# Another order of projections, and five set waits of the recurrence, in a two-layer hybrid decoder on one Trainium2 core

## The chip, the cores and the metric

The kernel runs on one core of one Trainium2 chip. TensorE (PE) multiplies matrices, VectorE (DVE), ScalarE (ACT) and GpSimd (POOL) work element by element, SyncE (SP) issues most of the transfers. The metric is the device time of one execution in microseconds, the median over several runs. Before the change it is 1106.13 us in three runs, from 1104.96 to 1108.74.

## The reference

Two layers work on x of 1024 positions by 1024 channels, both conditioned on one vector c. The first layer, in which the change lies, has one input projection whose columns feed two groups, and one output projection:

```python
p = h @ w_in                                  # r, k, v, w_lo, a_lo | u, v_g | z
# group A, 8 heads of 64: for each position t
sa  = S @ (-kk_t)
S   = S * w_t + sa (kk_t * a_t)^T + v_t k_t^T
y_t = S @ r_t                                 # then a layer norm per head, + bonus * v
# group B, 8 groups of 64: a spatial gate in chunks of 128 positions
y_b = u * (W_s @ layernorm(v_g) + b_s)
y   = concat(y_a, y_b) * silu(z) @ w_out
x   = x + gate * y
```

The second layer is attention in a window of 128 positions with its own projections, and a last RMSNorm follows.

## The kernel before

**Projections.** All weights and activations of the projections are split into a rounded part and a remainder, so that one tile of 128 output channels by 512 positions (a half of the sequence) takes 8 x 3 = 24 matmuls into one PSUM buffer, pproj. A column tile of the first layer is numbered: 0 to 3 are r of the head pairs 0 to 3, 4 to 7 are k, 8 to 11 are v, 12 the low-rank inputs of decay and a, 13 to 16 u, 17 to 20 the v of the spatial gate (called gv here), 21 to 24 the gate z of group A, 25 to 28 the gate of group B (zg). The stream (lines 989 to 1011) goes through them in the tuple ORDER (line 987), both halves of each, 24 matmuls a half. Tile 12 and pair 0 come ahead of it in the kernel's first part; three of their second halves open the stream, which makes 72 + 25 x 48 = 1272 matmuls. For the next tile in the order SP fetches the weights, ACT and POOL split them, while the one before is multiplied.

**Rooms.** After a half's matmuls the stream asks for room before the tile is evicted: r, k and v need fewer than 6 tiles held (line 981), z fewer than 2 waiting, gv fewer than 2 long-lived tiles, u fewer than 2. Where there is no room, the stream stands still. A unit (one head pair, one half of the sequence; eight of them, unit = 2 x pair + half) gives back its three tiles in front(): k behind the product with f, r behind AR, v behind bv.

**The recurrence's threads.** A unit runs through front (line 559: decay and low-rank products lw and la, the norm of kk by the transposes kt and kb, then BK, AR, SV, the transposes bkt and an, the bonus product bon), solve (line 664: products A, then on DVE a triangular solve of 15 steps that ends in ZT, then products p and pM with the steps M, Tq, M1), prep (line 776: products uw, mq and pn), scan (line 807: seven or eight hops of the state, product py) and post (line 834). front of a unit may begin when its r, k and v are there and solve of the unit before it has done its A products (line 1025). The spatial gate has its own thread, gm_tail (line 870: product gvn, a norm with vn on DVE, lnb, bst on DVE, product mix), and another thread accumulates the conditioning vectors of the second layer on DVE (adacc).

**Who sets the order on PE.** When the kernel is built, a planner (drive, line 1174) keeps a clock of its own. Each thread issues a few matmuls and then yields a time in microseconds: it may go on when the planner's clock has passed that time. The clock advances by a cost of each matmul, 512/2400 us for one of the stream. Among threads that are ready the lowest rank goes first: scan, then prep, solve and post, then front, gm_tail, the conditioning thread, and last the stream, which fills what is left; a debt lets the stream go first when the others have used much. The result is one fixed order of PE's instructions. On the chip PE executes it in that order and stands wherever an operand isn't ready. The waits of the threads are entries of the table LAT (line 58): 'unit_norm' between kt and kb, 'uw' between uw and mq, 'qt4' ahead of the product of N21 with Tq. Between la and kt, and between mq and pn, there is no wait. The instructions of the other engines are put in order by a scheduler with a model of times.

**What ends the stage.** When the stream is done and the other threads are nearly done, the output projection begins (out0_thread, line 1118).

Of the kernel before, what the change touches and what calls it, by code (L numbers as in the profile page):

```python
# [56 lines left out]

LAT = {"debt": 0.7, "share": 0.4, "p1": 2.31, "uw": 3.0, "mq": 4.0, "f0": 0.5, "sv0": 4.0, "wo": 2.31, "x1": 6.0, "yf": 7.85, "fetch": 3.85, "unit_norm": 12.0, "c81": 4.0, "qt1": 1.5, "bkt": 1.0, "qt2": 20.0, "qt3": 1.65, "qt4": 1.77, "qt5": 1.2, "qt6": 1.0, "yn": 12.0, "gm_tail1": 1.0, "gm_tail2": 12.0, "lnb": 1.0, "do_ada1": 4.5, "pick1": 0.5, "hop": 1.3, "ada": 8.0}

# [34 lines left out]
def tile_kernel(ctx, tc, x, cons, par, rows, ada, ada0, ew, wup, sgw, sgb, ewo, ow, owo, out, dbg=None):  # L94
# [43 lines left out]
    def pm(name):  # L138
        return ps.tile([P, HT], F32, name=name, tag="m", bufs=2)
# [419 lines left out]
    def front(un):  # L559
        j, half = un // 2, un % 2  # L560
# [26 lines left out]
        E2 = L  # L587
        S.activation(E2, L, AF.Exp, scale=KAPPA)
        pt = pm("kt")
        for b in range(4):  # L590
            transpose(pt[:, b * P:(b + 1) * P], kkn[:, b * P:(b + 1) * P], ident)
        sq = tmp("sqk")
        norm_scale(pt, sq, 1e-24, None, ALU.max, ALU.bypass, "k", rt)
        yield LAT["unit_norm"]
        pb = pm("kb")
# [30 lines left out]
        solvable[0] = un + 1  # L626
        yield LAT["f0"]
        SV = utile(un, [P, 8, 2, 64], "SV")
# [7 lines left out]
        S.activation(SV[0:64, 1:8:2, 1, :], pv4[64:128, :, 1, :], AF.Copy)  # L636
        yield LAT["c81"]
        BR = utile(un, [P, 8, 2, 2, 64], "BR")
        for g in range(2):
            pt = pm("bkt")  # L640
            for i in range(4):
                transpose(pt[:, i * P:(i + 1) * P], BK[:, g * 4 + i, :], ident)
            yield LAT["bkt"]
            S.activation(BR[:, g * 4:g * 4 + 4, :, 0, :], pt.rearrange("p (c e k) -> p c e k", c=4, e=2), AF.Copy)
        PA = utile(un, [P, 8, 2, 64], "PA")
        pt = pm("an")
        for i in range(4):
# [16 lines left out]
    def solve(un):  # L664
        AR, BK = us[un]["AR"], us[un].pop("BK")
        yield LAT["sv0"]
        yield lambda: scannable[0] > un
# [11 lines left out]
        for g in range(2):  # L679
            cg = slice(g * 4, g * 4 + 4)  # L680
            pts = [pm("A"), pM()]
            for i in range(4):
                c = g * 4 + i
                for hd in range(2):
                    hs = rows2[hd]
                    mm(pts[hd][:, i * P:(i + 1) * P], lhsT=BK[hs, c, :], rhs=AR[hs, :, c, :], start=True, stop=True)
            for hd in range(2):
                os = rows2[1 - hd]
                p4 = pts[hd].rearrange("p (c t) -> p c t", t=P)
                V.tensor_tensor(out=BR[:, cg, hd, 1, :], in0=p4[:, :, 64:128], in1=mr4, op=ALU.mult)  # L690
                V.tensor_tensor(out=AV[os, cg, :], in0=p4[os, :, 0:64], in1=ma4[os], op=ALU.mult)
                b0 = hd * 64
                for qd in range(2):
                    rows = slice(b0 + qd * 32, b0 + qd * 32 + 32)
                    ac = qd * 32
                    S.activation(Dgv[rows, cg, :, :], p4[rows, :, ac:ac + 32].rearrange("p c (b t) -> p c b t", b=2), AF.Copy)
                S.activation(N21[b0:b0 + 32, cg, :], p4[b0:b0 + 32, :, 32:64], AF.Copy)
            yield LAT["qt1"]

# [23 lines left out]
        Df = Dg.rearrange("p x t -> p (x t)")  # L723
        yield LAT["p1"]
        pt = pm("p1")
# [3 lines left out]
        S.activation(PA[:, :, 0, :], pt.rearrange("p (c v) -> p c v", c=8), AF.Copy)  # L729
        yield LAT["qt2"]  # L730
        p1 = pM()
# [6 lines left out]
        S.activation(M0, p1[:, 0:256].rearrange("p (c t) -> p c t", t=32), AF.Copy)  # L738
        yield LAT["qt3"]
        for c in range(8):  # L740
# [9 lines left out]
        for qd in range(4):  # L750
# [4 lines left out]
            else:  # L755
                S.activation(Z[rs, :, zc:zc + 32], Zq[rs], AF.Copy)
        yield LAT["qt4"]
        p1 = pM()
# [7 lines left out]
        S.activation(M1[96:128], p1v[96:128, :, 0:32], AF.Copy)  # L766
        yield LAT["qt5"]
        for c in range(8):
# [4 lines left out]
        S.activation(Z[64:96, :, 96:128], p1v[64:96, :, 32:64], AF.Copy)  # L773
        yield LAT["qt6"]

    def prep(un):
        u = us[un]
        AR, SV, BR, PA, dC = (u[k] for k in ("AR", "SV", "BR", "PA", "dC"))
        for g in range(2):
            cg = slice(g * 4, g * 4 + 4)  # L780
            pt = pm("uw")
            for i in range(4):
                mm(pt[:, i * P:(i + 1) * P], lhsT=Z[:, g * 4 + i, :], rhs=PA[:, g * 4 + i, :, :], start=True, stop=True)
            p4 = pt.rearrange("p (c a v) -> p c a v", c=4, a=2)
            S.activation(PA[:, cg, 1, :], p4[:, :, 1, :], AF.Copy)
            S.activation(SV[0:64, cg, 0, :], p4[0:64, :, 0, :], AF.Copy)
            S.activation(SV[64:128, cg, 1, :], p4[64:128, :, 0, :], AF.Copy)
        wdone[0] = un + 1
        yield LAT["uw"]
        for g in range(2):  # L790
            cg = slice(g * 4, g * 4 + 4)
            pt = pm("mq")
            for i in range(4):
                for e, hs in enumerate(rows2):
                    mm(pt[hs, i * P:(i + 1) * P], lhsT=PA[hs, g * 4 + i, 1, :], rhs=BR[hs, g * 4 + i, e, :, :], start=True, stop=True)
            p4 = pt.rearrange("p (c a v) -> p c a v", c=4, a=2)
            for e, hs in enumerate(rows2):
                V.tensor_tensor(out=Z[hs, cg, hs], in0=p4[hs, :, 0, :], in1=i2[hs].unsqueeze(1).to_broadcast([64, 4, 64]), op=ALU.add)
            V.tensor_tensor(out=AR[:, 1, cg, :], in0=p4[:, :, 1, :], in1=AR[:, 1, cg, :], op=ALU.add)
        pn = pm("pn")  # L800
        for c in range(8):
            for e, hs in enumerate(rows2):
                mm(pn[hs, c * 64:c * 64 + 64], lhsT=BR[:, c, e, 0, :], rhs=SV[:, c, e, :], start=True, stop=True)
        V.tensor_tensor(out=PA[:, :, 0, :], in0=pn.rearrange("p (c v) -> p c v", c=8), in1=dC.unsqueeze(2).to_broadcast([P, 8, 64]), op=ALU.mult)
        yield LAT["mq"]

    def scan(un):
        half, u = un % 2, us[un]
        AR, SV, BR, PA, dC = (u[k] for k in ("AR", "SV", "BR", "PA", "dC"))
        if half:  # L810
            V.tensor_copy(PA[:, 0, 1, :], Sst)
        else:
            V.tensor_copy(PA[:, 1, 1, :], PA[:, 0, 0, :])
        yield LAT["hop"]
        pc = psc("chain")
        for c in range(1 - half, 8 - half):
            yc = slice(c * 64, c * 64 + 64)
            mm(pc[:, yc], lhsT=Z[:, c, :], rhs=PA[:, c, 1, :], start=True, stop=True)
            if c == 7 - half:
                hopped[0] = un + 1  # L820
            V.scalar_tensor_tensor(out=PA[:, c + 1, 1, :] if c < 7 else Sst, in0=pc[:, yc], scalar=dC[:, c:c + 1], in1=PA[:, c, 0, :], op0=ALU.mult, op1=ALU.add)
            if c == 4:
                py = ps.tile([P, HT], F32, name="py", tag="y", bufs=1)
                for i in range(8):
                    for e, hs in enumerate(rows2):
                        mm(py[hs, i * 64:i * 64 + 64], lhsT=BR[:, i, e, 1, :], rhs=SV[:, i, e, :], start=i == 0, stop=False)
            if c < 7:
                yield LAT["hop"]
        for c in range(1 - half, 8):
            for hs in rows2:  # L830
                mm(py[hs, c * 64:c * 64 + 64], lhsT=AR[hs, 1, c, :], rhs=PA[hs, c, 1, :], start=False, stop=c == 7)
        return py

    def post(un, py):
        j, bv = un // 2, us[un]["bv"]
        sq = tmp("sqy", "tp", 2)
        norm_scale(py, sq, 1.0 / 64, LNX_EPS, ALU.mult, ALU.add, "y", lp)
        yield LAT["yn"]
        pb = pm("yt")
# [30 lines left out]
    def gm_tail(j, half, vT):  # L870
        if half == 0:
            gmc[j] = gm_consts(j)
        sgwt, lnb, bst = gmc[j]
        yield LAT["gm_tail1"]
        if half == 0:
# [14 lines left out]
        V.tensor_tensor(out=vg, in0=pv.rearrange("p (a d) -> p a d", d=64), in1=rs.unsqueeze(2).to_broadcast([P, 8, 64]), op=ALU.mult)  # L890
        yield LAT["gm_tail2"]
        yield lambda: (j, half) in gated_u
        if half == 0:
# [3 lines left out]
            V.tensor_tensor(out=bst, in0=pb[:, 0:P], in1=bst, op=ALU.add)  # L897
            yield LAT["lnb"]
        ut = gated_u.pop((j, half))
# [86 lines left out]

    ORDER = (21, 5, 1, 9, 17, 13, 6, 2, 22, 10, 25, 18, 7, 3, 23, 11, 14, 26, 24, 19, 15, 27, 20, 16, 28)

    def stream():
# [8 lines left out]
        while todo:  # L998
# [10 lines left out]
            if todo:  # L1009
                w = wn  # L1010
        done["h1"] = new_h()

    def prioritised(gen, offset):
# [468 lines left out]
```

## Time and profile before

| what | us |
|---|---|
| median of 3 runs | 1106.13 |
| the profiled execution, own time | 1109.73 |
| its span from first to last instruction | 1107.6 |
| PE busy | 1040.8 |
| DVE busy | 696.3 |
| ACT busy | 524.3 |
| POOL busy | 374.7 |

In the trace the first layer's overlapped stage, in which stream, recurrence and spatial gate share PE, lies from about 78 us to about 620 us from the span's start; the output projection of the first layer follows up to about 735 us, the second layer fills the rest. Times of instructions below are counted from the span's start. A row of a timeline is start, duration, engine, line, operation, output and inputs with the shape, how many instructions are merged in it, and in brackets how long the engine stood before it and what ended that. Matmuls overlap, so their pace is read from the distance of their starts.

### The profile page before, as it was taken

How to read it: one execution, taken by the hardware profiler on the slowest of the kernel's cores; microseconds unless marked ns; L12 is line 12 of the kernel's file. 1: busy time of each engine (PE TensorE's matmuls, PEld its weight loads, DVE VectorE, ACT ScalarE, POOL GpSimd, SP SyncE). 2: the span in 40 equal slices, each digit the busy share in tenths (PEclk: the TensorE clock that was granted, in tenths of full speed). 3: DMA queues.
4: the chain of work that ended last, by engine and by line, in shares of the span. 5: the costliest groups of instructions: out<-in, count | busy, mean ns of one | idle time of the engine just before them, and what ended most of it. 6: DMA issues, size and time to landing. Idle time of an engine off the chain costs nothing. (4 is left out here: it accounts for less than half of the span.)

```text
span 1107.6 us, 20700 instructions
## 1 busy us (share of the span) xinstructions
PE 1040.8 (94%) x7887; PEld 839.4 (76%) x7888; DVE 696.3 (63%) x1668; ACT 524.3 (47%) x1247; POOL 374.7 (34%) x483
## 2 busy tenths in 40 slices
PE   6989999999988898989999899999999999999997
PEld 3667778777776676766878777778888888878886
DVE  4455958586859485595642578864565654488754
ACT  4465555454454435445332233335565654487521
POOL 2333315141335122263423100134554544467201
PEclk9989999999999899999999899999999999999999
DMA  9501121212112121123122554421110111252121
GB/s 365 224 17 39 58 77 49 68 49 77 58 61 69 46 86 58 40 79 113 60 79 74 188 183 153 156 68 39 39 39 20 39 39 39 63 176 72 63 95 58
DMA packets 55131, 93.42 MB, mean 84 GB/s; under 512 B 5748, under 2 KB 15988, under 8 KB 55032
## 3 DMA queue, kind: packets, MB, share of 16 engines
q1 hardware_dynamic: 45176, 77.36, 21.3%
q10 hardware_dynamic: 9856, 14.75, 4.2%
q8 instruction: 62, 1.02, 0.4%
q14 instruction: 37, 0.30, 0.1%
HBM read 79.49 MB, written 12.59 MB: 83 GB/s over the span
## 5 line engine op out<-in xcount | busy, mean ns | idle before, releaser
L118 PE MATMUL pproj<-lo,whi 128*128 128x512 f32 x696 | 281.2, 404 | 0.0
L118 PE MATMUL pproj<-hi,whi 128*128 128x512 f32 x696 | 279.5, 402 | 0.7 <-ACT vt L1247 0.7
L118 PE MATMUL pproj<-hi,wlo 128*128 128x512 f32 x696 | 279.7, 402 | 0.0
L246 POOL TENSOR_TENSOR wlo<-wraw,whi 128x512 fp32r<-128x512 f32 x86 | 113.8, 1343 | 167.5 <-ACT whi L245 166.5
L118 PEld LDWEIGHTS pproj<-lo,whi 128*128 128x128 f32 x696 | 131.6, 189 | 24.9 <-issue 1.5
L118 PEld LDWEIGHTS pproj<-hi,whi 128*128 128x128 f32 x696 | 131.5, 189 | 24.5 <-ACT vt L1247 1.1
L118 PEld LDWEIGHTS pproj<-hi,wlo 128*128 128x128 f32 x696 | 131.3, 189 | 24.5 <-issue 1.2
L245 ACT ACTIVATE whi<-wraw 128x512 fp32r<-128x512 f32 x102 | 58.7, 622 | 65.9 <-PE htp L122 22.1
L118 PE MATMUL op<-wo,whi 128*128 128x512 f32 x256 | 82.2, 402 | 0.0
L1283 ACT ACTIVATE Sx<-Sx,nm 128x257 f32<-128x257 f32 (+1 forms) x128 | 62.3, 489 | 27.6 <-DVE nm L1279 25.5
L1279 DVE CUSTOM_DVE_ANT_0 Sx<-pS,bias,nsink 128x256 f32<-128x256 f32 (+1 forms) x128 | 53.4, 463 | 30.1 <-PE pS L118 28.6
L1287 POOL TENSOR_SCALAR Sx<-Sx,rc 128x256 f32<-128x256 f32 (+1 forms) x128 | 60.8, 492 | 25.4 <-DVE rc L1285 22.9
L1299 DVE TENSOR_TENSOR PL<-pT,PH 128x512 fp32r<-128x512 f32 (+1 forms) x64 | 41.6, 654 | 29.7 <-ACT PH L1298 29.2
L118 PEld LDWEIGHTS op<-wo,whi 128*128 128x128 f32 x256 | 49.0, 192 | 13.0 <-issue 2.1
L925 DVE SCALAR_TENSOR_TENSOR adacc<-araw,cond,adacc 128x512 f32<-128x512 f32 x56 | 44.0, 786 | 18.5 <-DMA araw<-ada 18.4
L118 PE MATMUL op<-hi,yh 128*128 128x512 f32 (+1 forms) x136 | 51.8, 381 | 0.4 <-ACT yh L1397 0.4
L118 PE MATMUL op<-hi,yl 128*128 128x512 f32 (+1 forms) x136 | 51.7, 380 | 0.4 <-DVE yl L1398 0.4
L118 PE MATMUL op<-wo,wlo 128*128 128x512 f32 x128 | 51.7, 404 | 0.0
L118 PE MATMUL op<-lo,yh 128*128 128x512 f32 (+1 forms) x136 | 51.5, 379 | 0.0
L213 POOL TENSOR_TENSOR st<-st,nhalf 128x1 f32<-128x1 f32 x16 | 9.6, 602 | 102.6 <-DVE st L212 91.0
L714 DVE TENSOR_TENSOR pr<-Lf,LT 128x2 f32<-128x2 f32 (+14 forms) x120 | 42.5, 354 | 2.7
L1298 ACT ACTIVATE PH<-pT 128x512 fp32r<-128x512 f32 (+1 forms) x64 | 35.7, 563 | 17.5 <-PE pT L1293 16.2
(317 smaller groups left out, 2166.5 us busy)
## 6 DMA issues: line engine op xcount, KB each, us to landing
araw<-ada SPq DMA_DIRECT2D x64, 256.0 KB, 2.8
wraw<-ew SPq DMA_DIRECT2D x50, 256.0 KB, 3.0
wraw<-ow SPq DMA_DIRECT2D x36, 256.0 KB, 3.0
adaraw<-ada SPq DMA_DIRECT2D x16, 512.0 KB, 9.0
x<-x SPq DMA_DIRECT2D x8, 512.0 KB, 8.7
woraw<-ewo SPq DMA_DIRECT2D x16, 256.0 KB, 2.9
xr<-x ACTq DMA_DIRECT2D x16, 256.0 KB, 3.5
wraw<-y0d SPq DMA_DIRECT2D x16, 256.0 KB, 3.1
```

Of the source, the lines that this page charges most:

```text
L118: last[0] = nc.tensor.matmul(out, lhsT=lhsT, rhs=rhs, **kw).ins
L213: G.tensor_tensor(out=st[:, 3:4], in0=st[:, 2:3], in1=nhalf[:, 0:1], op=ALU.pow)
L245: a = S.activation(hi[:, gs, :], raws[g], AF.Copy)
L246: b = E.tensor_tensor(out=lo[:, gs, :], in0=raws[g], in1=hi[:, gs, :].bitcast(F32), op=ALU.subtract)
L714: V.tensor_tensor(out=pr[:, 0:nc_, 0:i + 1], in0=Lf[:, i:i + 1, 0:i + 1].to_broadcast([P, nc_, i + 1]), in1=LTt[:, 0:nc_, 0:i + 1], op=ALU ...
L925: op = V.scalar_tensor_tensor(out=acc, in0=raw, scalar=cond[:, k:k + 1], in1=acc, op0=ALU.mult, op1=ALU.add)
L1279: V.tensor_tensor_reduce(out=Sx[:, e, off:2 * P], in0=pS3[:, e, 0:nk], in1=bias[e][:, off:], scale=1.0, scalar=nsink[:, hd:hd + 1], op0=AL ...
L1283: S.activation(pr[:, e, off:2 * P + 1], Sx[:, e, off:2 * P + 1], AF.Exp, bias=nm[:, e:e + 1], scale=-1.0, accum_out=sm[:, e:e + 1])
L1287: G.tensor_scalar(out=pr[:, e, off:2 * P], in0=pr[:, e, off:2 * P], scalar1=rc[:, e:e + 1], scalar2=0.5, op0=ALU.mult, op1=ALU.mult)
L1298: S.activation(PH[:, ks, :], pT2[:, ks, :], AF.Copy)
L1299: V.tensor_tensor(out=PL[:, ks, :], in0=pT2[:, ks, :], in1=PH[:, ks, :].bitcast(F32), op=ALU.subtract)
```

## The change

Three things. The tuple ORDER gets k, r and v of the pairs 1 to 3 without a gated tile among them: u of pair 0 moves from before k of pair 2 to behind z of pair 1, v of pair 2 moves ahead of z 1, v of pair 3 ahead of z 2, gv of pair 1 moves from before k 3 to behind z 2. From the 841st matmul on the order is the same as before. Two waits of LAT get other values: uw 3.0 to 2.0, qt4 1.77 to 2.3. A second table MORE adds to the waits per unit, and functions lat() and opt() read both; it holds three entries, with the same value for all eight units: 1.0 more between la and kt, 0.7 more between mq and pn, 1.5 more in unit_norm. The other calls of opt() ('an', 'mq1', 'py', 'pa') have no entry and yield nothing, and the other calls of lat() give what LAT gave. No instruction is added or removed.

```diff
-LAT = {..., "uw": 3.0, ..., "qt4": 1.77, ...}
+LAT = {..., "uw": 2.0, ..., "qt4": 2.3, ...}
+MORE = {
+    "kt": (1.0, 1.0, 1.0, 1.0, 1.0, 1.0, 1.0, 1.0),
+    "pn": (0.7, 0.7, 0.7, 0.7, 0.7, 0.7, 0.7, 0.7),
+    "unit_norm": (1.5, 1.5, 1.5, 1.5, 1.5, 1.5, 1.5, 1.5),
+}
...
         S.activation(E2, L, AF.Exp, scale=KAPPA)
+        yield from opt("kt", un)
         pt = pm("kt")
...
-        yield LAT["unit_norm"]
+        yield lat("unit_norm", un)
...
-        yield LAT["qt4"]
+        yield lat("qt4", un)
...
-        yield LAT["uw"]
+        yield lat("uw", un)
...
+        yield from opt("pn", un)
         pn = pm("pn")
...
-    ORDER = (21, 5, 1, 9, 17, 13, 6, 2, 22, 10, 25, 18, 7, 3, 23, 11, 14, 26, 24, 19, 15, 27, 20, 16, 28)
+    ORDER = (21, 5, 1, 9, 17, 6, 2, 10, 22, 13, 25, 7, 3, 11, 23, 18, 14, 26, 24, 19, 15, 27, 20, 16, 28)
...
+    def lat(name, un):
+        return LAT.get(name, 0.0) + MORE.get(name, (0.0,) * 8)[un]
+
+    def opt(name, un):
+        if name in MORE and MORE[name][un]:
+            yield MORE[name][un]
```

More of the change, by code (lines that the diff above doesn't have):

```diff
@@ L55 @@
 NC2 = CONSTS["alibi"]
-LAT = {"debt": 0.7, "share": 0.4, "p1": 2.31, "uw": 3.0, "mq": 4.0, "f0": 0.5, "sv0": 4.0, "wo": 2.31, "x1": 6.0, "yf": 7.85, "fetch": 3.85, "unit_norm": 12.0, "c81": 4.0, "qt1": 1.5, "bkt": 1.0, "qt2": 20.0, "qt3": 1.65, "qt4": 1.77, "qt5": 1.2, "qt6": 1.0, "yn": 12.0, "gm_tail1": 1.0, "gm_tail2": 12.0, "lnb": 1.0, "do_ada1": 4.5, "pick1": 0.5, "hop": 1.3, "ada": 8.0}
+LAT = {"debt": 0.7, "share": 0.4, "p1": 2.31, "uw": 2.0, "mq": 4.0, "f0": 0.5, "sv0": 4.0, "wo": 2.31, "x1": 6.0, "yf": 7.85, "fetch": 3.85, "unit_norm": 12.0, "c81": 4.0, "qt1": 1.5, "bkt": 1.0, "qt2": 20.0, "qt3": 1.65, "qt4": 2.3, "qt5": 1.2, "qt6": 1.0, "yn": 12.0, "gm_tail1": 1.0, "gm_tail2": 12.0, "lnb": 1.0, "do_ada1": 4.5, "pick1": 0.5, "hop": 1.3, "ada": 8.0}
+MORE = {
[3 more added lines that the diff above has]
+}
 def _consts():
@@ L626, in front @@
         solvable[0] = un + 1
-        yield LAT["f0"]
+        yield lat("f0", un)
         SV = utile(un, [P, 8, 2, 64], "SV")
@@ L636, in front @@
         S.activation(SV[0:64, 1:8:2, 1, :], pv4[64:128, :, 1, :], AF.Copy)
-        yield LAT["c81"]
+        yield lat("c81", un)
         BR = utile(un, [P, 8, 2, 2, 64], "BR")
@@ L642, in front @@
                 transpose(pt[:, i * P:(i + 1) * P], BK[:, g * 4 + i, :], ident)
-            yield LAT["bkt"]
+            yield lat("bkt", un)
             S.activation(BR[:, g * 4:g * 4 + 4, :, 0, :], pt.rearrange("p (c e k) -> p c e k", c=4, e=2), AF.Copy)
         PA = utile(un, [P, 8, 2, 64], "PA")
+        yield from opt("an", un)
         pt = pm("an")
@@ L665, in solve @@
         AR, BK = us[un]["AR"], us[un].pop("BK")
-        yield LAT["sv0"]
+        yield lat("sv0", un)
         yield lambda: scannable[0] > un
@@ L697, in solve @@
                 S.activation(N21[b0:b0 + 32, cg, :], p4[b0:b0 + 32, :, 32:64], AF.Copy)
-            yield LAT["qt1"]
+            yield lat("qt1", un)
         solving[0] = un + 1
@@ L723, in solve @@
         Df = Dg.rearrange("p x t -> p (x t)")
-        yield LAT["p1"]
+        yield lat("p1", un)
         pt = pm("p1")
@@ L729, in solve @@
         S.activation(PA[:, :, 0, :], pt.rearrange("p (c v) -> p c v", c=8), AF.Copy)
-        yield LAT["qt2"]
+        yield lat("qt2", un)
         p1 = pM()
@@ L738, in solve @@
         S.activation(M0, p1[:, 0:256].rearrange("p (c t) -> p c t", t=32), AF.Copy)
-        yield LAT["qt3"]
+        yield lat("qt3", un)
         for c in range(8):
@@ L766, in solve @@
         S.activation(M1[96:128], p1v[96:128, :, 0:32], AF.Copy)
-        yield LAT["qt5"]
+        yield lat("qt5", un)
         for c in range(8):
@@ L773, in solve @@
         S.activation(Z[64:96, :, 96:128], p1v[64:96, :, 32:64], AF.Copy)
-        yield LAT["qt6"]
+        yield lat("qt6", un)
     def prep(un):
@@ L788, in prep @@
         wdone[0] = un + 1
-        yield LAT["uw"]
+        yield lat("uw", un)
         for g in range(2):
             cg = slice(g * 4, g * 4 + 4)
+            if g:
+                yield from opt("mq1", un)
             pt = pm("mq")
@@ L804, in prep @@
         V.tensor_tensor(out=PA[:, :, 0, :], in0=pn.rearrange("p (c v) -> p c v", c=8), in1=dC.unsqueeze(2).to_broadcast([P, 8, 64]), op=ALU.mult)
-        yield LAT["mq"]
+        yield lat("mq", un)
     def scan(un):
@@ L813, in scan @@
             V.tensor_copy(PA[:, 1, 1, :], PA[:, 0, 0, :])
-        yield LAT["hop"]
+        yield lat("hop", un)
         pc = psc("chain")
@@ L822, in scan @@
             if c == 4:
+                yield from opt("py", un)
                 py = ps.tile([P, HT], F32, name="py", tag="y", bufs=1)
@@ L827, in scan @@
             if c < 7:
-                yield LAT["hop"]
+                yield lat("hop", un)
+        yield from opt("pa", un)
         for c in range(1 - half, 8):
@@ L837, in post @@
         norm_scale(py, sq, 1.0 / 64, LNX_EPS, ALU.mult, ALU.add, "y", lp)
-        yield LAT["yn"]
+        yield lat("yn", un)
         pb = pm("yt")
@@ L873, in gm_tail @@
         sgwt, lnb, bst = gmc[j]
-        yield LAT["gm_tail1"]
+        yield lat("gm_tail1", 2 * j + half)
         if half == 0:
@@ L890, in gm_tail @@
         V.tensor_tensor(out=vg, in0=pv.rearrange("p (a d) -> p a d", d=64), in1=rs.unsqueeze(2).to_broadcast([P, 8, 64]), op=ALU.mult)
-        yield LAT["gm_tail2"]
+        yield lat("gm_tail2", 2 * j + half)
         yield lambda: (j, half) in gated_u
@@ L897, in gm_tail @@
             V.tensor_tensor(out=bst, in0=pb[:, 0:P], in1=bst, op=ALU.add)
-            yield LAT["lnb"]
+            yield lat("lnb", 2 * j + half)
         ut = gated_u.pop((j, half))
```

## The prediction

> **What bounds the kernel now.** I read the page first, then the stages, then TensorE's waits, then TensorE's instructions in order of time around each wait.
>
> The page and the view of stages (span of the stage, then busy time and instructions of each engine, granted clock, DMA share, GB/s):
>
> ```profile
> span 1107.6 us, 20700 instructions
> PE 1040.8 (94%) x7887; PEld 839.4 (76%) x7888; DVE 696.3 (63%) x1668; ACT 524.3 (47%) x1247; POOL 374.7 (34%) x483
> ```
>
> ```profile
> 109.65:163.84 54.19, 50.76 (x517) 39.98 (x516) 39.46 (x87) 27.29 (x62) 14.01 (x11) 1.00 0.20 60
> 332.31:424.44 92.13, 82.81 (x926) 66.41 (x925) 65.45 (x159) 38.04 (x88) 26.26 (x23) 0.96 0.22 66
> ```
>
> The program has one order of instructions on PE, fixed when it is built. PE is busy 94% of the span, so time can be saved only where it stands. In the first layer's overlapped stage (78 to 620 us) it stands more in some stretches than in others: 3.4 us of 54 in the first row, 9.3 of 92 in the second.
>
> What it stood for (waiter, released by, total us, times, longest):
>
> ```profile
> PE kt L122 <- ACT th L573: 5.5, 7, 0.8
> PE pn L118 <- DVE AR L799: 5.1, 8, 0.8
> PE pM L118 <- DVE ZT L719: 4.6, 2, 3.0
> PE pM L118 <- ACT M L766: 3.4, 4, 1.8
> PE mix L118 <- DVE bst L897: 3.3, 1, 3.3
> PE mix L118 <- DVE vn L890: 3.3, 1, 3.3
> PE pM L118 <- DVE Tq L746: 1.9, 4, 0.7
> PE uw L118 <- ACT SV L787: 1.1, 1, 1.1
> ```
>
> All of these belong to this stage. Two kinds are to be told apart: small waits that come back in every unit (kt, pn, Tq), and single long ones (ZT, M, bst, uw) where other work stood in front on DVE or ACT.
>
> Which thread ends the stage (the instructions in order of time; start, duration):
>
> ```profile
> 595.63 1.15 PE L118 MATMUL py<-PA,AR 64*64 64x64 f32 x32
> 614.34 0.39 PE L118 MATMUL pproj<-hi,wlo 128*128 128x512 f32 x1
> 617.99 1.98 PE L118 MATMUL mix<-sgwt,vn 128*64 128x128 f32 x16 [3.26 <-DVE vn L890]
> ```
>
> The last unit's recurrence is over at 596.8, the stream of projections at 614.7. So the recurrence isn't what ends the stage: the sum of PE's work and its idle time is. A recurrence that is ready earlier gains nothing by that alone; a wait that is filled with a projection matmul moves the stream's end forward by its length, as long as projections are left, and 18 us of them are left behind the recurrence.
>
> What runs behind a wait (two of them, and the matmuls that followed):
>
> ```profile
> 431.76 0.69 PE L118 MATMUL pM<-Zq,M 32*32 32x32 f32 x32 [1.80 <-ACT M L766]
> 432.98 0.63 PE L118 MATMUL pproj<-lo,whi 128*128 128x512 f32 x1
> 433.41 0.63 PE L118 MATMUL pproj<-hi,wlo 128*128 128x512 f32 x1
> 434.69 1.58 PE L118 MATMUL uw<-PA,Z 128*128 128x128 f32 x8
> 501.05 0.75 PE L118 MATMUL pM<-ZT,Dg 16*32 16x32 f32 x64 [1.60 <-DVE ZT L719]
> 502.31 0.40 PE L118 MATMUL pproj<-hi,wlo 128*128 128x512 f32 x1
> 502.55 0.39 PE L118 MATMUL pproj<-hi,whi 128*128 128x512 f32 x1
> ```
>
> After 1.80 us of idling the projection matmuls start 0.43 us apart, up to 436.3; after 1.60 us they start 0.24 apart, which is the pace of the stage.
>
> **The change, part by part. Set wait before kt, +1.0 us, 8 units.** The planner counts a projection matmul as 512/2400 = 0.213 us, so 1.0 us puts five of them between la and kt. At 0.24 us each, five are 1.2 us. The longest wait is 0.8. All of it goes: −5.5 us. The matmuls aren't added work; they are taken from later.
>
> **Set wait before pn, +0.7.** Four matmuls, 0.96 us, over waits of at most 0.8: −5.1.
>
> **qt4 1.77 to 2.3.** Two or three matmuls more (0.5 to 0.7 us) ahead of the product that waits for Tq, whose longest wait is 0.7: −1.7 of 1.9.
>
> **unit_norm 12 to 13.5 and uw 3.0 to 2.0.** The first puts seven matmuls more ahead of kb, whose waits are too small for the lines above: 0. The second takes five away ahead of mq:
>
> ```profile
> 148.72 0.38 ACT L787 ACTIVATE SV<-uw 64x256 f32<-64x256 f32 x1
> 151.20 1.96 PE L118 MATMUL mq<-BR,PA 64*64 64x128 f32 x32
> ```
>
> The last eviction of uw ends at 149.10, 2.1 us ahead of mq; five matmuls are 1.2, so 0.9 is still covered: 0. Without that cover each unit would pay what is missing. None of these waits is one of an engine's: nothing queues behind it on the chip. On PE other threads' instructions stand there instead, and the front's own steps come some 3 us later in the stream.
>
> Sum of the set waits: −5.5 − 5.1 − 1.7 = −12.3.
>
> **The order of the stream.** First where the recurrence waits for its tiles. Ends of A (pM x2) and the next unit's first product (lw):
>
> ```profile
> 270.68 0.38 PE L118 MATMUL pM<-AR,BK 64*128 64x128 f32 x2
> 288.39 0.69 PE L118 MATMUL lw<-lora,wupt 64*128 64x512 f32 x1
> 391.68 0.38 PE L118 MATMUL pM<-AR,BK 64*128 64x128 f32 x2
> 424.44 0.69 PE L118 MATMUL lw<-lora,wupt 64*128 64x512 f32 x1
> ```
>
> Unit 4's front could begin at 271 by its other condition (A of unit 3 done) and begins at 288; unit 6's at 392 and begins at 424. Their v tiles are the last of their pairs and come then. With r, k and v moved ahead of the gated tiles, unit 4 begins near 272, unit 6 near 393 (v of pair 3 takes the 697th to 744th place instead of the 793rd to 840th), and the recurrence ends some 40 us earlier. By the paragraph above that is worth nothing directly. It matters by what then meets on DVE and ACT: gv 1 moves from the 601st to the 793rd place, so its tail's norm no longer lies in unit 4's triangular solve, and unit 6's solve comes ahead of the tails of pair 1 rather than among them; front 6 no longer starts in unit 5's last solve steps. Waits of those meetings: ZT 4.6, bst 3.3, the largest M 1.8, uw 1.1, together 10.8. I count half, −5.4, as the other half can return with other neighbours: ends 0 and −10.8.
>
> **The clock behind long waits.** The slow stretch above, 432.4 to 436.3, is 3.9 us at near half speed and loses about 1.7 us (an estimate from these rows). Three such waits (3.0, 1.8, 3.3) lie in the meetings above: 5.1 at most, half again: −2.5. [...]
>
> **What the order adds.** A projection whose tile has no free buffer stops the stream. Buffers come free one by one; the projections done by then (instructions of pproj from 78.1 on; the count follows PE's time):
>
> ```profile
> 78.10:220.60 142.50, 94.22 (x366) 65.78 (x366) 8.06 (x11) 10.58 (x18) 1.00 0.19 57
> 78.10:235.17 157.07, 103.54 (x400) 71.72 (x400) 8.80 (x12) 11.53 (x20) 1.00 0.19 56
> 78.10:246.25 168.15, 111.48 (x429) 76.87 (x429) 9.54 (x13) 12.22 (x21) 1.00 0.18 54
> 78.10:394.60 316.50, 192.11 (x721) 128.96 (x722) 16.68 (x23) 20.70 (x36) 0.99 0.19 58
> 78.10:616.00 537.90, 338.49 (x1272) 228.25 (x1272) 26.06 (x37) 35.93 (x62) 0.99 0.21 66
> ```
>
> The stream is 1272 matmuls, 24 a tile. The 720th, unit 6's half of v in the new order, is done by 394.6, so front 6 can start there. v of pair 2 takes the 409th to 456th place now; its halves need unit 3's r freed (behind kb, 235.17, 400 done) and unit 3's v freed (behind bon, 246.25, 429 done): 32 and 27 matmuls to spare. The set waits eat most of that, 5 + 4 + 2.5 − 5 = 6.5 a unit for two units, and 12 more in unit 3's own front: about 25. A stop of a few matmuls is likely. I charge 1.5 us for it, and 1.5 for units 3 and 5, whose solves get a front beside them for the first time: +3. Weight fetches on SP, their splits on ACT and POOL and the constants of gv 1 on ACT's queue move with their tiles; the order of issue and use stays, so 0. The end of the stage (3.3 for vn) keeps its order: 0.
>
> **Sum.** −12.3 − 5.4 − 2.5 + 3 = −17.2. The profiled execution took 1109.73 us (span 1107.6 and 2.1 around it), 3.6 above the median of the three runs, 1106.13. Span 1107.6 to 1090.4, own time to 1092.5, median 1106.13 to 1088.9: **1089**.
>
> **Rivals.**
>
> Only the set waits count (0.22). The recurrence isn't the end, so the order moves tiles and long waits alike. −12.3 and half of the 3: 1095. For it: the last row of the end. Against: the long waits lie where tails and a late front meet a solve.
>
> The solves pay (0.11). Products p of units 3 and 4, and their ZT:
>
> ```profile
> 276.53 1.15 PE L118 MATMUL p<-SV,AV 64*64 64x64 f32 x32
> 288.83 0.42 DVE L719 TENSOR_TENSOR ZT<-Tm,rcon 128x256 f32<-128x256 f32 x1
> 335.52 1.15 PE L118 MATMUL p<-SV,AV 64*64 64x64 f32 x32
> 361.10 0.41 DVE L719 TENSOR_TENSOR ZT<-Tm,rcon 128x256 f32<-128x256 f32 x1
> ```
>
> Unit 3, with no front beside it, had ZT 12.7 us after p; unit 4, with front 5 and a tail, 26.0. PE comes back about 22 us after p. Units 3 and 5 now get a front. If both came out like unit 4 they would wait 3.0 each and 1.7 for the clock, 9.4 together, the order's gain gone: −12.3 + 9.4, 1103. Against: unit 1 had a front and a DVE busy 39.46 of 54.19 us, and the list has two ZT waits in eight units. What lengthens such a chain is seen here:
>
> ```profile
> 344.18 1.36 DVE L714 TENSOR_TENSOR pr<-Lf,LT 128x45 f32<-128x45 f32 x1
> 229.80 0.25 DVE L714 TENSOR_TENSOR pr<-Lf,LT 128x45 f32<-128x45 f32 x1
> 344.14 2.54 POOL L246 TENSOR_TENSOR wlo<-wraw,whi 128x512 fp32r<-128x512 f32 x2
> ```
>
> The same product takes 1.36 us beside a split on POOL and 0.25 elsewhere. [...]
>
> The stream stops at its rooms (0.08), and the kernel is slower. From kt to kb of unit 3 the stream gives 34 matmuls (366 to 400; 8.2 us); a tile that stands there for the whole of it leaves PE without them: 8.2 and 1.7 for the clock, 9.9 a tile. It decides from the third tile on: 17.2 + 3.3 is 20.5, and three are 29.7: 1119. Against: by the counts two tiles only come near their room; for pair 3 the rooms are free long before.
>
> **How the numbers follow.** The forecast's mechanism has 0.59; its own range is 1078 (all meetings gone, nothing added: −12.3 − 10.8 − 5.1 = −28.2) to 1097. A measurement of this kernel tells 0.3%, 3.3 us, from no change. Forecast and first rival are faster, 0.81, with the edge of the second 0.82; the rest of the second is the same, 0.10; the third slower, 0.08. Low 1078, high 1102 leaves out the third rival, most of the second and the forecast's edges: 2 in 10.
>
> **What would show it.** kt, pn and Tq gone from TensorE's waits or under 1 us together; front 4 beginning near 272 and front 6 near 390; the last py 30 to 45 us ahead of the stream's end where it was 18; ZT, bst and M under 6 us in total. Wrong would be: new waits of over 2 us at ZT in units 3 or 5, PE standing before a krv tile's projection, or a stage end that moved by less than 8 us although kt and pn are gone.

## The result, and the profile after

After the change the median is 1095.04 us (4 executions, 1091.82 to 1096.67), beside 1106.47 us for the kernel before on the same chip (4 executions): ratio 0.9891, interval 0.9863 to 0.9920. The forecast was 1089.0 with 1078 to 1102 around it. The profiled execution of after took 1095.26 us, its span is 1093.2.

The overlapped stage, from 78 us to the first matmul of the output projection, in the view of stages (stage, length, busy time of PE, PEld, DVE, ACT, POOL, granted clock, DMA share, GB/s), first before:

```profile
78.00:619.89 541.89, 501.29 (x5112) 398.71 (x5110) 354.46 (x813) 251.19 (x562) 177.26 (x140) 0.98 0.22 67
```

and after:

```profile
78.00:603.82 525.82, 498.86 (x5093) 394.10 (x5092) 357.22 (x810) 247.70 (x560) 173.25 (x139) 0.99 0.22 68
```

The stage is 16.1 us shorter. PE's idle time in it (length less busy) goes from 40.6 to 27.0, its busy time from 501.3 to 498.9. Behind the stage 1.7 us are given back, so that the span is 14.4 shorter. 1.1 of them are the last product mix, which stood ahead of the output projection's first product op before (617.99, op at 619.89) and now stands behind five of its matmuls (605.54, op at 603.82).

TensorE's waits after:

```profile
PE bkt L127 <- DVE BK L614: 6.6, 4, 2.8
PE chain L123 <- DVE PA L831: 6.1, 9, 1.4
PE pM L123 <- DVE Tq L753: 4.9, 4, 2.6
PE bkt L127 <- ACT qh L619: 1.9, 1, 1.9
PE gvn L123 <- DVE mx L917: 1.6, 1, 1.6
PE pM L123 <- ACT M L745: 1.4, 1, 1.4
PE pM L123 <- DVE ZT L726: 0.3, 1, 0.3
```

and two rows of before that the prediction did not show:

```profile
PE chain L118 <- DVE PA L821: 3.3, 4, 1.2
PE bkt L122 <- DVE BK L608: 0.8, 1, 0.8
```

Gone are kt (5.5), pn (5.1), bst (3.3), vn (3.3), both waits of uw (1.1 and 1.4), 4.3 of ZT and 2.0 of M (3.4 at one step of the solve, L766 of before, are gone; 1.4 at an earlier step, L745 of after, are new): 26.0 us. New are bkt (+7.7), Tq (+3.0, where a decrease was forecast), chain (+2.8) and gvn (+1.4, from 0.2): 14.9. Waits of 3.3 us for adag (at 657.5 and 708.5) lie in the output projection and are not in these sums.

Fronts of units 4 and 6, the last product of the recurrence and the end of the stream, in order of time:

```profile
274.50 0.69 PE L123 MATMUL lw<-lora,wupt 64*128 64x512 f32 x1
389.54 0.69 PE L123 MATMUL lw<-lora,wupt 64*128 64x512 f32 x1
559.75 1.15 PE L123 MATMUL py<-PA,AR 64*64 64x64 f32 x32
603.60 0.39 PE L123 MATMUL pproj<-hi,wlo 128*128 128x512 f32 x1
603.82 0.62 PE L123 MATMUL op<-wo,whi 128*128 128x512 f32 x2
```

Units 4 and 6 begin 14 and 35 us earlier, and the recurrence ends 43 us ahead of the stream where it was 18. Still, the end is set by PE's work and its waits.

**Where the new bkt waits come from.** On after's DVE, around the end of unit 0's triangular solve, with front of unit 1 beside it:

```profile
135.43 0.43 DVE L726 TENSOR_TENSOR ZT<-Tm,rcon 128x256 f32<-128x256 f32 x1
135.89 0.45 DVE L729 STREAM_TRANSPOSE Zq<-ZT 128x256 f32<-128x256 f32 x1
136.26 0.68 DVE L625 SCALAR_TENSOR_TENSOR AR<-kkn,E 128x504 f32<-128x504 f32 x1
...
137.62 1.66 DVE L614 SCALAR_TENSOR_TENSOR BK<-kkn,tha 64x512 f32<-64x512 f32 x1
```

and the PE instruction that waits for it:

```profile
139.43 1.09 PE L127 MATMUL bkt<-con,BK 128*128 128x128 f32 x4 [2.77 <-DVE BK L614]
```

The same steps of the kernel before:

```profile
128.62 1.47 DVE L619 SCALAR_TENSOR_TENSOR AR<-kkn,E 128x504 f32<-128x504 f32 x1
...
131.10 1.68 DVE L608 SCALAR_TENSOR_TENSOR BK<-kkn,tha 64x512 f32<-64x512 f32 x1
134.58 0.42 DVE L719 TENSOR_TENSOR ZT<-Tm,rcon 128x256 f32<-128x256 f32 x1
```

Before, front's AR and BK stood among the solve's products and ZT behind them; in unit 4, where they stood at 351.0 to 356.5 and ZT at 361.1, PE waited 2.99 us for ZT. After, ZT and Zq come first and PE waits for BK. It is the same DVE time in another order: a wait for the solve was traded for a wait for the front.

**The clock.** The view of stages over the stretches in which the granted clock was low (the last but two column), before:

```profile
358.00:370.00 12.00, 8.19 (x152) 6.25 (x151) 5.76 (x16) 4.87 (x12) 1.79 (x2) 0.72 0.15 45
430.00:438.00 8.00, 5.11 (x50) 4.40 (x51) 4.54 (x9) 4.68 (x11) 3.85 (x3) 0.79 0.12 35
482.00:490.00 8.00, 7.76 (x46) 6.27 (x47) 6.90 (x17) 2.37 (x6) 4.01 (x2) 0.79 0.33 103
614.00:619.89 5.89, 2.63 (x20) 1.87 (x18) 3.75 (x6) 1.23 (x2) 3.58 (x3) 0.73 0.74 239
```

and after:

```profile
138.00:146.00 8.00, 6.57 (x86) 5.41 (x87) 5.44 (x8) 4.65 (x11) 2.00 (x2) 0.59 0.15 42
574.00:578.00 4.00, 3.58 (x15) 3.41 (x16) 2.55 (x4) 1.67 (x4) 1.21 (x2) 0.59 0.67 213
```

Length times what is missing from 1 is the loss: 3.4, 1.7, 1.7 and 1.6 before, 3.3 and 1.6 after. The same view, over 360.70 to 367.52, 432.38 to 435.79, 483.58 to 486.99 and 616.70 to 623.52 us of before and over 137.79 to 144.62 and 574.70 to 578.11 of after, has the clock at 0.50 throughout: 3.41 us, or twice that, so that the loss comes in pieces of 1.7 us in this stage of the two traces (the last stretch of before runs past its end at 619.89). Each of these stretches lies at a wait, of 2.99, 1.80, 3.26 and 3.26 us before; after's two begin at the bkt wait above (2.77 us) and at a gvn wait of 1.61 us. A part of it lies in the wait itself (0.50 already from 138.0 to 139.4, ahead of bkt), so that loss and idle time do not simply add. In windows of 4 us over the whole stage the loss is 8.3 before and 5.1 after.

### The profile page after: what moved, and what is told of

Its sections match the earlier page's. It is cut to its first block, busy times and chain, and to the rows that moved or that the text cites. A ratio compares the mean times of both kernels' runs of the same rounds, so it can differ in the third digit from the quotient of the medians.

```text
span 1093.2 us, 20714 instructions
## 1 busy us (share of the span) xinstructions
PE 1036.7 (95%) x7888; PEld 833.8 (76%) x7888; DVE 701.3 (64%) x1668; ACT 521.4 (48%) x1247; POOL 372.5 (34%) x483
## 5 line engine op out<-in xcount | busy, mean ns | idle before, releaser
L250 ACT ACTIVATE whi<-wraw 128x512 fp32r<-128x512 f32 x102 | 59.0, 624 | 56.0 <-issue 18.5
L123 PEld LDWEIGHTS op<-wo,whi 128*128 128x128 f32 x256 | 48.1, 188 | 12.4 <-issue 1.0
L937 DVE SCALAR_TENSOR_TENSOR adacc<-araw,cond,adacc 128x512 f32<-128x512 f32 x56 | 50.6, 903 | 8.8 <-DMA araw<-ada 8.7
```

What stands on the lines that cost most here:

```text
L123: last[0] = nc.tensor.matmul(out, lhsT=lhsT, rhs=rhs, **kw).ins
L250: a = S.activation(hi[:, gs, :], raws[g], AF.Copy)
L937: op = V.scalar_tensor_tensor(out=acc, in0=raw, scalar=cond[:, k:k + 1], in1=acc, op0=ALU.mult, op1=ALU.add)
```

## The experiments

All kernels were timed against the kernel before, whose median was 1106.93 to 1107.60 in these runs; the row of after is that of the result, against 1106.47. The columns: ratio with its interval; the clock, as the median over all timed executions; then of the profiled execution the stage's length from 78 us, PE's idle time in it (length less busy), the number of PE waits of 1.5 us or more in it, and the clock loss in windows of 4 us.

| kernel | ratio | median us | clock | stage | idle | long waits | clock loss |
|---|---|---|---|---|---|---|---|
| before | 1 | 1107 | 0.988 to 0.990 | 541.9 | 40.6 | 5 | 8.3 |
| after | 0.9891 [0.9863, 0.9920] | 1095.0 | 0.989 | 525.8 | 27.0 | 5 | 5.1 |
| order alone | 0.9940 [0.9922, 0.9958] | 1100.4 | 0.990 | 529.8 | 34.4 | 3 | 3.4 |
| five waits alone | 0.9939 [0.9924, 0.9954] | 1099.8 | 0.987 | 529.3 | 28.6 | 6 | 10.1 |
| kt and pn alone | 1.0035 [1.0022, 1.0048] | 1110.9 | 0.980 | 542.3 | 38.1 | 9 | 11.1 |
| kt alone | 1.0051 [1.0031, 1.0072] | 1112.4 | 0.981 | 542.8 | 40.2 | 9 | 10.6 |
| pn alone | 0.9982 [0.9971, 0.9993] | 1105.1 | 0.984 | 537.7 | 38.7 | 6 | 3.5 |
| unit_norm, uw, qt4 alone | 1.0096 [1.0077, 1.0116] | 1118.5 | 0.983 | 550.2 | 45.8 | 6 | 11.4 |
| after without kt, pn | 1.0020 [1.0006, 1.0034] | 1108.8 | 0.987 | 542.2 | 41.0 | 5 | 10.2 |
| after without unit_norm | 0.9960 [0.9943, 0.9977] | 1103.5 | 0.982 | 530.3 | 27.3 | 7 | 11.9 |
| kt, pn and yn 18.5 | 1.0129 [1.0109, 1.0149] | 1123.2 | 0.979 | 549.0 | 41.7 | 8 | 15.4 |
| after, LT filled by DVE | 0.9892 [0.9865, 0.9918] | 1093.2 | 0.990 | 523.7 | 25.6 | 5 | 3.4 |
| after, eight waits more | 0.9877 [0.9863, 0.9890] | 1092.9 | 0.988 | 524.1 | 23.4 | 4 | 3.4 |
| after, both of these | 0.9888 [0.9866, 0.9909] | 1094.0 | 0.989 | 522.6 | 24.5 | 4 | 3.4 |

**The order alone**: ORDER as in the change, LAT as before, no MORE.

```diff
-    ORDER = (21, 5, 1, 9, 17, 13, 6, 2, 22, 10, 25, 18, 7, 3, 23, 11, 14, ...)
+    ORDER = (21, 5, 1, 9, 17, 6, 2, 10, 22, 13, 25, 7, 3, 11, 23, 18, 14, ...)
```

> The new order of the stream alone, all waits as before. Theory A (the order takes tails and the late front out of the solves; the set waits fill kt and pn but push the fronts against the solves): ZT, bst and vn waits of before (4.6, 3.3, 3.3 us) nearly gone, kt 5.5 and pn 5.1 still there, bkt under 2 us; 7 to 10 us faster, about 1098. Theory B (only the set waits count, the recurrence isn't the end of the stage): within 3 us of before, long waits replaced by others.

**The five waits alone**: the order of before with the change's LAT and MORE.

```diff
-    ORDER = (21, 5, 1, 9, 17, 6, 2, 10, 22, 13, 25, 7, 3, 11, 23, 18, 14, ...)
+    ORDER = (21, 5, 1, 9, 17, 13, 6, 2, 22, 10, 25, 18, 7, 3, 23, 11, 14, ...)
```

> All five set waits, the old order. Theory A: kt and pn gone (10.6 us), but bkt waits of 4 us or more and larger Tq waits come in, and ZT and mix stay as before: 2 to 6 us faster, about 1102. Theory B: the sum of the set waits in full, 12 us faster, about 1094, as fast as the whole change.

Each brings about 0.6%, and 0.9940 x 0.9939 is 0.988: between these two groups the gains add up. Both came outside what was expected of them: 6.7 us faster for the order where 7 to 10 or at most 3 stood, 7.3 for the waits where 2 to 6 or 12 stood. What each removes is not what the prediction said. The order alone leaves kt at 5.8 and pn at 4.9, and ZT at 5.3:

```profile
PE pM L118 <- DVE ZT L719: 5.3, 2, 2.8
```

The two waits are not those of before (2.99 in unit 4, 1.60 in unit 6). Unit 4's is still there with 2.54 us, and a new one came in unit 5, whose solve has the next front beside it for the first time:

```profile
417.89 0.75 PE L118 MATMUL pM<-ZT,Dg 16*32 16x32 f32 x64 [2.81 <-DVE ZT L719]
```

The waits of the five set waits alone:

```profile
PE bkt L127 <- DVE BK L614: 4.2, 2, 2.8
PE mix L123 <- DVE vn L902: 3.3, 1, 3.3
PE pM L123 <- DVE ZT L726: 2.9, 2, 2.6
PE mix L123 <- DVE bst L909: 2.5, 1, 2.5
```

The order takes away the two waits of mix. The set waits take away part of ZT, since they push front's AR and BK behind it, and leave mix.

**kt and pn alone**, in the order of before: the two waits that each hid over 5 us in the prediction.

```diff
-LAT = {..., "uw": 2.0, ..., "qt4": 2.3, ...}
+LAT = {..., "uw": 3.0, ..., "qt4": 1.77, ...}
-    "unit_norm": (1.5, 1.5, 1.5, 1.5, 1.5, 1.5, 1.5, 1.5),
```

> The two waits before kt and pn alone, old order, unit_norm, uw and qt4 as before. If each filled wait is worth its length: 10.6 us less idling and 10 to 11 us faster, about 1096. If the time is given back by other waits behind it (as the whole change shows at bkt and Tq): kt and pn gone, but 4 to 6 us faster only.

**kt alone, and pn alone**: the same, with one of the two entries.

```diff
 MORE = {
     "kt": (1.0, 1.0, 1.0, 1.0, 1.0, 1.0, 1.0, 1.0),
-    "pn": (0.7, 0.7, 0.7, 0.7, 0.7, 0.7, 0.7, 0.7),
 }
```

> The old order and only the wait ahead of kt (+1.0). Theory, that a shift of front by five matmuls changes what meets on DVE and ACT and this outweighs the 5.5 us of kt: the waits for kt are gone, pn stays at about 5, the waits for Tq, bkt or N grow by 5 us or more and the ratio is 1.000 to 1.006. Rival, that the wait ahead of pn is what gives it back: kt alone brings its 5.5 us, ratio 0.993 to 0.997.

> The old order and only the wait ahead of pn (+0.7). Theory (the shift of front is what gives it back): pn's waits go, kt stays at 5.5, nothing else moves much, ratio 0.994 to 0.997. Rival, that pn's wait, which puts the scan behind it later, is what gives it back: the waits for pn are gone, chain or the next unit's solve waits by as much, ratio 1.000 to 1.005.

kt and pn together are slower than before, where both expectations had them 4 to 11 us faster, and it is kt that does it. Waits of kt alone:

```profile
PE pM L121 <- DVE Tq L751: 5.4, 4, 3.2
PE pn L121 <- DVE AR L806: 5.4, 8, 1.0
PE bkt L125 <- DVE BK L612: 4.3, 3, 2.2
```

kt's seven waits are gone, as meant, and Tq and bkt have grown by 3.5 each. The sum of the idle time is what it was (40.2 beside 40.6), but seven waits of at most 0.8 us are gone and waits of 1.6 to 3.2 us at Tq and bkt have come: nine long ones instead of five. In twelve executions the clock lay between 0.972 and 0.986, the span between 1106.9 us (at 0.986) and 1118.5 (at 0.973). Between these two ends the clock's loss (span times what is missing from 1) grows by 14.7 us and the span by 11.6. The median clock, 0.981 beside 0.988 to 0.990, is 8 to 10 us more of such loss than before, and the kernel is 5.6 us slower by its ratio. A straight line through the twelve clocks and spans gives 1105.2 us at a clock of 0.988, an estimate a little beyond their range; before's 23 executions beside them have 1105.5 us and 0.988 in the median. So the clock, not the idle time, carries the slowdown of kt alone. pn alone leaves kt at 5.5 and brings 0.2%, less than expected: its 5.1 us go, but the idle time falls by only 1.9, and the clock is 0.984.

**What stands in front of Tq.** With kt and pn alone, DVE in unit 2 (bv of L859 and gz are steps of post, another thread):

```profile
248.70 0.75 DVE L859 SCALAR_TENSOR_TENSOR bv<-yc,der,bv 128x512 f32<-128x512 f32 x1 [2.79 <-ACT yc L858]
249.37 0.28 DVE L750 TENSOR_TENSOR Zq<-Zq,pM 128x128 f32<-128x128 f32 x1
249.56 1.66 DVE L1063 SCALAR_TENSOR_TENSOR gz<-bv,der,gz 128x512 f32<-128x512 f32 x1
251.26 1.54 DVE L760 COPY Z<-Zq 32x256 f32<-32x256 f32 x2
252.81 0.45 DVE L752 STREAM_TRANSPOSE Tq<-Zq 128x256 f32<-128x256 f32 x1
```

In before Zq, Z and Tq came first (Tq at 250.27) and bv behind them. Zq's other input, pM, ended at 248.2 (matmuls from 247.48 for 0.73 us), but Zq starts only behind bv, which waited 2.79 us for ACT, and gz's 1.66 us lie between Zq and Z: Tq comes at 252.81, 2.5 us later than in before. The theory was that this gives the gain back; the experiment puts post behind the solve again.

```diff
-LAT = {..., "yn": 12.0, ...}
+LAT = {..., "yn": 18.5, ...}
```

> The old order, the waits ahead of kt and pn as in the run with these two alone (ratio 1.0035 there, waits for Tq 8.7 us in five units), and post's wait 'yn' 12.0 to 18.5, by which post's two steps on DVE, bv and gz, stand behind Tq in seven of eight units (ahead of it or between its inputs in three or four before). Theory, that these two steps in front of Tq are what gave the gain of kt and pn back: the waits for Tq fall from 8.7 to under 2 us and the ratio from 1.0035 to 0.996 to 0.999. Rival, that each shift of a thread only deals the waits out anew: Tq falls, but other waits of 5 us or more take its place and the ratio stays at 1.001 to 1.006.

The theory fell, and beyond its rival, which had 1.001 to 1.006: 1.0129. Where bv had stood ahead of Tq, the waits fell to 0.8 us or vanished. But Tq's sum is still 5.1, with this in unit 5's solve, where steps of the next unit's front (the scan L, and BK at 431.5) and of the conditioning thread (adacc) stand in its place:

```profile
427.59 1.23 DVE L584 TENSOR_TENSOR_SCAN L<-smask,th 128x512 f32<-128x512 bf16 x1 [1.20 <-ACT th L582]
429.75 1.79 DVE L936 SCALAR_TENSOR_TENSOR adacc<-araw,cond,adacc 128x512 f32<-128x512 f32 x1
433.46 0.28 DVE L750 TENSOR_TENSOR Zq<-Zq,pM 128x128 f32<-128x128 f32 x1
434.38 0.45 DVE L752 STREAM_TRANSPOSE Tq<-Zq 128x256 f32<-128x256 f32 x1
```

and the PE instruction behind it:

```profile
434.97 0.69 PE L122 MATMUL pM<-Tq,N 32*32 32x32 f32 x32 [3.41 <-DVE Tq L752]
```

The single wait is rightly explained; removing its cause deals the others out anew.

**unit_norm, uw and qt4 alone**, in the order of before, and **after without kt and pn**:

```diff
 MORE = {
-    "kt": (1.0, 1.0, 1.0, 1.0, 1.0, 1.0, 1.0, 1.0),
-    "pn": (0.7, 0.7, 0.7, 0.7, 0.7, 0.7, 0.7, 0.7),
     "unit_norm": (1.5, 1.5, 1.5, 1.5, 1.5, 1.5, 1.5, 1.5),
 }
```

> unit_norm, uw and qt4 alone with the old order, without the waits before kt and pn. The prediction had 1.7 us for these three: 1105. All five in the old order took 7.3 us off and kt and pn alone added 3.7; if the two groups add up, these three are worth 11 us, 1096; if kt and pn pay only together with them, 1102 to 1106, with kt and pn waits of 10 us still in the list.

> The whole change without the waits before kt and pn (new order, unit_norm, uw and qt4). Theory P: kt and pn are worth 10.6 us, so 1105. Theory D (they are worth little, as alone in the old order): within 4 us of the whole change, 1092 to 1099, kt and pn waits of 10 us in the list and bkt, Tq and chain lower by about as much.

**After without unit_norm's 1.5**:

```diff
-    "unit_norm": (1.5, 1.5, 1.5, 1.5, 1.5, 1.5, 1.5, 1.5),
```

> The whole change without the 1.5 us more in unit_norm. Theory D (a set wait ahead of the front's steps is worth what it does to the order on VectorE: with unit_norm longer, the front's BK stands behind the solve's ZT, so ZT no longer waits and bkt does): bkt waits fall under 3 us from 8.5, ZT waits of 3 us or more come back, or Tq grows; 2 to 6 us slower than the whole change, 1097 to 1101. Theory P (the prediction's: unit_norm is worth 0): 1095, within 2 us.

The three entries priced at nothing or little cost 1.0% alone, 1118.5 us where the expectations had 1096 to 1106. Against before, idle time rises by 5.2 us, and the clock falls to 0.983. Yet with kt and pn beside them the five bring 0.6%, and without unit_norm the new order and the other four lose most of what they brought (0.9960), at the same idle time as after (27.3 and 27.0) but seven long waits and a clock of 0.982; bkt falls from 8.5 to 2.4 and Tq rises from 4.9 to 7.1, as expected, but the loss is larger than the 2 to 6 us that were expected. Without kt and pn the new order and the other three give 1.0020, 1108.8 us: the theory that these two are worth little there (1092 to 1099) fell. In the full change they are worth some 14 us (idle 27.0 with them, 41.0 without), more than the 10.6 of their own waits, where alone in the old order they cost 0.35%. If the parts added up, the five in the old order would cost 5.6 − 2.0 + 10.6 us (from the ratios of kt, pn and the three) = +14; they bring 7. The order, by contrast, is worth much the same whichever waits are set: 0.6% alone, 0.8% beside these three (1.0096 to 1.0020), 0.5% beside all five (0.9939 to 0.9891).

**LT filled by DVE.** In after, ACT stood 7.33 us at the fill of LT (it waits for the solve before to be done with it), with front's kkn queued behind; the theory was that this holds BK up. The edit puts the fill on DVE's own queue.

```diff
-        S.activation(LT.rearrange("p a b -> p (a b)"), RC("lt16", 128), AF.Copy)
+        V.tensor_copy(LT.rearrange("p a b -> p (a b)"), RC("lt16", 128))
```

> The whole change, and the fill of LT for the next unit's solve moved from ScalarE to VectorE, where the transpose that it must wait for runs anyway. Theory A: the new bkt waits (8.5 us) come from ScalarE standing before that fill (23.9 us) with kkn queued behind it; kkn comes 2 to 5 us earlier, bkt waits fall under 3 us and the kernel is 4 to 7 us faster than the whole change, about 1089. Theory C (bkt waits because VectorE is full): bkt waits stay, within 2 us of 1095, or a little slower by eight more copies on VectorE.

The theory fell: bkt's waits for BK stay.

```profile
PE bkt L127 <- DVE BK L614: 7.5, 5, 2.3
```

In unit 1 front's kkn is ready at 131.5 instead of 136.2, and this BK still starts at 138.28 (137.62 in after), behind ZT, Zq, AR and its own first half. ACT's stand was a stand beside the path; there BK's place in DVE's order is what counts.

**Eight waits more, by the trace of after**, and **both edits together**:

```diff
 MORE = {
     ...
+    "c81": (0.0, 2.5, 1.7, 1.3, 0.0, 1.2, 0.0, 1.1),
+    "qt4": (0.0, 0.0, 0.0, 1.6, 0.0, 2.4, 0.0, 0.0),
 }
```

> The whole change, and its new waits filled by the same means: the wait before bkt longer by 2.5, 1.7, 1.3, 1.2 and 1.1 us in units 1, 2, 3, 5 and 7, the wait before Tq's product by 1.6 and 2.4 in units 3 and 5. If a filled wait is worth its length: bkt and Tq waits of 13 us gone, 8 to 11 us faster than the whole change, about 1086. Theory D (the waits are VectorE's queue and come back behind the step that is moved): they fall, others rise by half or more of it, 0 to 4 us faster, about 1093.

> After, with both small edits that gave a slightly lower ratio each: eight set waits by the trace of after (c81 and qt4; ratio 0.9877) and the fill of LT on DVE (0.9892). Theory, that what remains are waits that come back elsewhere as soon as one is filled: ratio 0.986 to 0.989, PE idle between 78 us and the output projection 22 to 26 us. Rival, that the two add up: 0.984 to 0.986, idle under 21.

bkt falls from 8.5 us to 1.7 and Tq from 4.9 to 1.6, but chain rises to 8.5, and M and uw come back (3.4 and 2.5). Idle time falls by 3.5 us where bkt and Tq fall by 10.1. Both edits together come out as the theory had it, idle 24.5 us in the expected 22 to 26. 0.9877, 0.9892 and 0.9888 all lie in the interval of after: no version here beats it by what a measurement can tell.

## Why the prediction was right, and where it was not

**The size.** −17.2 was forecast for the span, −14.4 came in the profiles and −11.4 in the medians. Sign and range held. The 6.1 us between 1088.9 and 1095.0 have two parts. 2.8 are the sum itself (a span of 1093.2 where 1090.4 was forecast), of which 1.7 are what is given back behind the stage, a term that the sum does not have. The other 3.4 (rounded) come from carrying the profiled execution's offset over to the median: it was 3.6 us above the median before, and 0.2 after. The clock may be part of that offset (the profiled execution of before had 0.983, the executions timed in the experiments 0.988 to 0.990 in the median), but this is not shown: two executions of before at 0.984 took 1107.5 and 1107.7 us beside a median of 1107.6. 1095 is also the number of the rival "Only the set waits count", but its mechanism is refuted: the order alone gives 0.9940.

**kt and pn, −10.6.** Both are gone from the list, so the effect on these two waits was right. That the term stands by itself was wrong: alone the two give 1.0035, and in the full change they are worth some 14 us. The prediction had said that the front's own steps come some 3 us later in the stream, and priced that at nothing; this is the step that failed. kt alone shows it: DVE's and ACT's orders change with PE's, and 5.5 us of short waits came back as long ones.

**qt4, −1.7.** Tq rose by 3.0 instead; of the signs that the prediction named, this is the one that did not come. **unit_norm and uw, 0.** Wrong for unit_norm: without it after loses 0.7%. No run has uw by itself.

**The meetings, half of 10.8.** ZT, bst, M and uw fell from 12.4 us (with all of M) to 1.7, nearly all of what was counted, and uw's other wait of 1.4 went too. But the order alone shows the reason given to hold only for bst, M and uw: it leaves ZT at 5.3, 2.5 of it in unit 4 as before and 2.8 in unit 5 in place of unit 6. The set waits alone leave 2.9 of it. ZT goes only when the set waits put front's steps behind it in the new order too, and bkt is the bill.

**The clock, −2.5.** In the two profiles −3.2; in the medians after's 0.989 beside 0.988 to 0.990 is no difference that these runs can show. The long waits were as many as before (five). The step rested on one execution whose clock was unusually low (0.983; the 57 executions of before in the experiments have 0.984 to 0.993). After lost clock too, in two stretches at 0.59, without a wait over 2.8 us in the stage; the longest of before is 3.26.

**The end of the stage, 0.** vn's 3.3 went, and the reason given, that the order there stays, was wrong. The recurrence ends 43 us ahead of the stream, so that the last unit's bv and gz no longer stand ahead of the gate's norm on DVE (611.5 to 613.5 before), and on PE five matmuls op now stand ahead of mix. The run with the order alone shows the wait gone and the same order of op and mix, the one with the waits alone shows it at 3.3; which of the two removes how much is not separated.

**What is added, +3.** This is the most mis-sized term: 14.9 of new waits. Of the two places that were named, the first did not happen: no two matmuls of the stream start further apart than 4.9 us, at the bkt wait of 2.77 (5.2 before), so that the stream stops nowhere for want of room. The second, the solves of units 3 and 5 with a front beside them, did happen, but at Tq: waits of 1.71 and 2.58 us, 4.3 where 1.5 were charged. In unit 5 front's AR and BK and post's bv stand between ZT (405.09) and Tq:

```profile
410.83 0.69 DVE L614 SCALAR_TENSOR_TENSOR BK<-kkn,tha 64x512 f32<-64x512 f32 x1
411.55 1.80 DVE L860 SCALAR_TENSOR_TENSOR bv<-yc,der,bv 128x512 f32<-128x512 f32 x1
414.88 0.45 DVE L753 STREAM_TRANSPOSE Tq<-Zq 128x256 f32<-128x256 f32 x1
```

With the order alone the same solve waits 2.81 us at ZT. So the rival "The solves pay" had this part right, though at 4.3 us and no loss of clock instead of 9.4. The other new waits are at bkt, chain and gvn. The terms that went beyond the forecast (5.3 at the meetings, 1.4 of uw, 3.3 of vn, some 2.5 of smaller waits: 12.5) and those that fell short (11.9 here, 1.7 of qt4: 13.6) nearly balance, which is why the total came close. That they do is luck: nothing in the prediction ties the one to the other.

**What stays open.** Why these five entries together are good, when each group alone is bad, was traced for single waits only. That the number of long waits sets the clock is argued from the comparison of the kernels; no run changed that number alone. The order on DVE and ACT follows from a scheduler's model, and no run gave all parts the same order on these engines.

## What to carry to other kernels

Where a fixed order on one engine is tuned by waits, a set wait is not a local edit: judge it together with its neighbours, and look in the trace of DVE and ACT for whose steps now stand in front of whose. Ask of a removed wait whether many short ones became a few long ones; with kt alone the idle time was the same (40.2 us beside 40.6), the clock 0.981 beside 0.988 to 0.990 and the kernel 5.6 us slower. And compare the profiled execution, its time and its clock, with other executions before its offset from the median or its loss of clock enters a sum.

## What the runs showed of the hardware

The clock loss came in pieces of 1.7 us (3.41 us at 0.50, or twice that, in the overlapped stage of before and after), and the length of a wait alone did not decide on it. After had this wait (its timeline) and this clock in the 4 us behind it (its view of stages):

```profile
415.47 0.69 PE L123 MATMUL pM<-Tq,N 32*32 32x32 f32 x32 [2.58 <-DVE Tq L753]
```

```profile
415.47:419.47 4.00, 4.00 (x76) 3.16 (x77) 0.00 (x0) 2.15 (x6) 0.00 (x0) 1.00 0.08 30
```

and the kernel with LT filled by DVE, at the same place of its program, in the same two views:

```profile
413.72 0.98 PE L123 MATMUL pM<-Tq,N 32*32 32x32 f32 x32 [2.59 <-DVE Tq L753]
```

```profile
413.72:417.72 4.00, 4.00 (x56) 2.96 (x58) 0.00 (x0) 1.13 (x3) 0.00 (x0) 0.57 0.08 30
```

2.58 us cost nothing, 2.59 cost 1.7 (4.00 us at 0.57). The clock of one kernel also differs from one execution to the next: 0.972 to 0.986 in twelve of kt alone. What decides whether such a wait costs clock is not shown. Over the kernels the clock falls with the number of long waits, counted in one execution of each: 0.988 to 0.990 with three to five (0.987 in one kernel with five), 0.983 to 0.987 with six, 0.982 with seven, 0.979 to 0.981 with eight or nine.
